# A hybrid SSD and forgetting-attention step on one core: weights times values in one fp32 product that also gives the sums, and row maxima from the high halves alone

## The chip, the cores and the metric

The kernel runs on one core of a Trainium2 chip. The metric is the device time of one execution in microseconds (us). The core has five engines that matter here: PE (matrix products; its weight loads are listed as PEld), DVE (vector), ACT (scalar functions), POOL (general purpose, also vector work) and the queues that issue DMA transfers, most of them on SP.

## The reference, cut to what matters

One inference step of a layer: a combined input projection, a Mamba-2 scan (8 heads) beside a forgetting attention (8 heads of 64), an output projection, a gated feed-forward part. The prompt has 2048 tokens, and 128 sample tokens (8 streams of 16) go with it. The change lies in the attention over the prompt, which is causal and has a per-token decay `F` added to the scores:

```python
def fox_block(q, k, v, fq, fk, q_pos, k_pos):
    s = jnp.einsum('bqhd,bkhd->bhqk', q, k).astype(jnp.float32) * FOX_SCALE
    s = s + (jnp.swapaxes(fq, 1, 2)[:, :, :, None] - jnp.swapaxes(fk, 1, 2)[:, :, None, :])
    s = jnp.where((k_pos[None, :] <= q_pos[:, None])[None, None], s, -jnp.inf)
    p = jax.nn.softmax(s, axis=-1)
    return jnp.einsum('bhqk,bkhd->bqhd', p.astype(v.dtype), v)
```

Everything is fp32.

## The kernel before

**Precision.** Most large products run in the format fp32r, on operands split into a high and a low half (`split`, L103 to L108: a cast to fp32r gives the high half, a subtraction the low one). A product of two split operands takes three fp32r products. A few small products (the scan's, L504, L511, L514, and transposes) run on plain fp32 operands.

**Stages.** The prompt goes through the input projection and the mixers in four parts of 512 tokens (p = 0 to 3). For each part `a_head` normalises, `a_body` projects (L116 to L118 and L346 to L348), and `attention(p, others)` runs the part's 8 heads, with chunks of the scan (`ssd_chunk`) between. The output projection (L819 to L821) begins while the attention of p = 3 runs. The feed-forward part (L116 to L118 with `wr`, L919 to L921) follows. The framework's scheduler decides in which order the instructions of these strands stand on each engine; each engine then runs its own list in order, and waits where something is not ready.

**Attention.** Scores of a block of 512 queries (`qb`) against a block of 512 keys (`kb`) are worked out twice.

- `s_phase` puts queries on the partitions, for the softmax's maximum and sum: for each of 4 groups of 128 queries two products (L589 over 128 rows, L590 over 68 rows: 64 dimensions and four rows for the decay and, later, the maximum), a maximum over the keys on DVE (L593), and an exponential with its sum on ACT (L594). At the end (L596 to L621) the maxima and sums of the blocks are joined, turned (L613), written to DRAM and read back: the maximum as two more rows of the queries, the reciprocal of the sum as `rdb`, spread over 64 partitions.
- `t_phase` puts keys on the partitions: for each of 4 groups of 128 keys two products (L646, L647), an exponential on ACT that gives the weights `pr` (L653), a split of the weights into `pp` by DVE (high, L107) and POOL (low, L108), and, two groups later, `weigh`: two products (L635) of the values with the high and with the low half of the weights. The stationary operand has the values' high half in 64 columns and their low half in the other 64, so the two halves of the accumulator `pv` are added at the end (L662, L663) and multiplied by `rdb` (L664).

Below, a unit is one such group of 128 keys (and beside it one of 128 queries): 8 heads times 4, 8, 12 and 16 units in the four parts, 320 in all. Of a head's diagonal block the four units are 512, 384, 256 and 128 columns wide, all others 512: 224 units of 512 and 32 each of 384, 256 and 128. `s_phase` runs ahead of `t_phase` by 4 units (`LEAD`), within one strand.

**Scan chunk.** `ssd_chunk` begins with `sg`, a difference of running sums for 8 heads, clipped at zero: 8 DVE instructions (L474), then an exponential.

## Time and profile before

| | |
|---|---|
| median of 3 runs | 3247.06 us (3239.56 to 3247.18) |
| the profiled execution, its time | 3243.1 us |
| its span, first to last instruction | 3241.4 us |
| PE busy | 3038.1 us (94%) |
| DVE, ACT, POOL busy | 2049.0, 1216.5, 1229.2 us |
| mean granted share of PE's clock | 0.969 |

The profile is of one execution. "Busy" of PE is the union of its instructions' spans, whose ends are modelled: a product of 512 columns lasts 0.39 us there while the next begins 0.23 us after it. The granted clock is the share of PE's full rate; it is either 1 (2.4 GHz) or 0.5 (1.2 GHz), and a value between is a mean over a stretch.

### The profile page before, as it was taken

To read this page: it belongs to the slowest core of one execution; us is meant where nothing else is said; L and a number is where in the kernel's file an instruction comes from. 1 tells how busy PE (TensorE), PEld (TensorE's weight loads), DVE (VectorE), ACT (ScalarE), POOL (GpSimd) and SP (SyncE) were. 2 spreads that over 40 slices of the span, in tenths; PEclk is the share of its full clock that TensorE was granted. 3 is DMA by queue.
4 is the path that set the end of the run, shared out by engine and by line. 5 is a ranking of instruction groups with operands and counts; after the bars stand their busy time and mean duration, and the time that the engine had idled before them with its cause. 6 is when DMAs were issued, how large, how long until landed. Compare 5 with 4: busy or idle time off the path is not lost.

```text
span 3241.4 us, 48271 instructions
## 1 busy us (share of the span) xinstructions
PE 3038.1 (94%) x18032; PEld 2741.7 (85%) x18032; DVE 2049.0 (63%) x3922; ACT 1216.5 (38%) x2442; POOL 1229.2 (38%) x803
## 2 busy tenths in 40 slices
PE   5988889799989997999899999999999999999999
PEld 5977788688878785886699999998999999999998
DVE  5376456867786777557555555556555555766666
ACT  3353344445555555434332222234222223322222
POOL 3343234554556556434333223233322323333332
PEclk9999989899989998998999999999999999999999
DMA  5767775676657656655432112123211212322221
GB/s 174 232 207 233 251 217 176 206 215 199 179 174 221 198 155 206 198 180 174 174 118 78 59 59 66 57 74 118 78 60 58 65 60 71 117 78 69 73 69 70
DMA packets 253458, 442.93 MB, mean 137 GB/s; under 512 B 24416, under 2 KB 121704, under 8 KB 253224
## 3 DMA queue, kind: packets, MB, share of 16 engines
q1 hardware_dynamic: 199656, 278.60, 27.6%
q10 hardware_dynamic: 53568, 161.24, 16.0%
q8 instruction: 143, 2.34, 0.3%
q14 instruction: 91, 0.75, 0.1%
HBM read 352.91 MB, written 86.84 MB: 136 GB/s over the span
## 4 chain that ended last, share of the span: by engine, by line
PE 70%; DMA 13%; DVE 10%; issue 3%; ACT 2%; POOL 2%; SPq 1%; ACTq 0%; DVEq 0%; POOLq 0%
PE mm L116 13%; PE mm L117 12%; PE mm L118 12%; PE dn L919 5%; PE dn L920 5%; PE dn L921 5%; PE pv L635 2%; DMA sg<-ac_d 2%; DVE pp L107 1%; PE dn L819 1%; PE dn L820 1%; PE dn L821 1%; DMA k<-k_d 1%; PE s L646 1%; PE s L589 1%
## 5 line engine op out<-in xcount | busy, mean ns | idle before, releaser
L108 POOL TENSOR_TENSOR wr<-raw,wr 128x1024 fp32r<-128x1024 f32 x198 | 475.9, 2411 | 1033.8 <-ACT wr L105 1025.5
L116 PE MATMUL mm<-nT,wr 128*128 128x386 f32 (+1 forms) x2112 | 697.0, 331 | 1.3 <-ACT wr L105 0.8
L117 PE MATMUL mm<-nT,wr 128*128 128x386 f32 (+1 forms) x2112 | 695.9, 330 | 0.1
L118 PE MATMUL mm<-nT,wr 128*128 128x386 f32 (+1 forms) x2112 | 695.2, 329 | 0.0
L108 POOL TENSOR_TENSOR pp<-pr,pp 128x512 fp32r<-128x512 f32 (+1 forms) x320 | 384.9, 1207 | 469.6 <-DVE pp L107 439.5
L897 DVE SCALAR_TENSOR_TENSOR ac<-mm,cw,ac 128x384 f32<-128x384 f32 (+1 forms) x528 | 301.8, 572 | 345.0 <-ACT ac L895 337.3
L895 ACT ACTIVATE ac<-mm,cw 128x384 f32<-128x384 f32 (+1 forms) x264 | 172.5, 653 | 786.5 <-PE mm L118 783.9
L922 DVE TENSOR_TENSOR y<-y,dn 128x512 f32<-128x512 f32 x374 | 255.4, 685 | 266.7 <-PE dn L921 263.9
L117 PEld LDWEIGHTS mm<-nT,wr 128*128 128x128 f32 x2112 | 399.9, 189 | 6.8 <-DVE nT L108 0.3
L116 PEld LDWEIGHTS mm<-nT,wr 128*128 128x128 f32 x2112 | 398.1, 189 | 7.7 <-ACT wr L105 1.1
L118 PEld LDWEIGHTS mm<-nT,wr 128*128 128x128 f32 x2112 | 398.3, 189 | 5.7
L108 POOL TENSOR_TENSOR cmw<-craw,cmw 128x1024 fp32r<-128x1024 f32 (+1 forms) x96 | 234.6, 2446 | 256.1 <-ACT cmw L105 237.9
L116 PE MATMUL mm<-nT,cmw 128*128 128x256 f32 (+2 forms) x1024 | 310.8, 303 | 16.8 <-DVE qk L405 5.5
L118 PE MATMUL mm<-nT,cmw 128*128 128x256 f32 (+2 forms) x1024 | 306.8, 300 | 0.0
L117 PE MATMUL mm<-nT,cmw 128*128 128x256 f32 (+2 forms) x1024 | 306.8, 300 | 0.0
L919 PE MATMUL dn<-wr,ht 128*128 128x512 f32 x748 | 294.6, 394 | 2.9 <-DVE y L922 1.7
L920 PE MATMUL dn<-wr,ht 128*128 128x512 f32 x748 | 293.0, 392 | 0.0
L921 PE MATMUL dn<-wr,ht 128*128 128x512 f32 x748 | 290.4, 391 | 0.0
L635 PE MATMUL pv<-pp,v 128*128 128x512 f32 (+3 forms) x640 | 231.4, 405 | 50.0 <-DVE yl L663 17.4
L105 ACT CAST wr<-raw 128x1024 fp32r<-128x1024 f32 x198 | 203.2, 1042 | 173.7 <-PE dn L921 161.4
L594 ACT ACTIVATE s<-s,nm 128x512 f32<-128x512 f32 (+2 forms) x320 | 190.9, 597 | 153.9 <-DVE nm L593 145.2
L653 ACT ACTIVATE pr<-s 128x512 f32<-128x512 f32 (+1 forms) x320 | 167.8, 532 | 182.3 <-PE s L647 118.4
(299 smaller groups left out, 6008.6 us busy)
## 6 DMA issues: line engine op xcount, KB each, us to landing
raw<-in_w_up ACTq DMA_DIRECT2D x132, 512.0 KB
k<-k_d SPq DMA_DIRECT2D x160, 256.0 KB
raw<-in_w_down ACTq DMA_DIRECT2D x66, 512.0 KB
craw<-in_w_cm ACTq DMA_DIRECT2D x64, 512.0 KB
k<-k_d SPq DMA_DIRECT2D x160, 136.0 KB
v<-v_d SPq DMA_DIRECT2D x80, 256.0 KB
craw<-in_w_tm ACTq DMA_DIRECT2D x24, 512.0 KB
q_d<-qk SPq DMA_DIRECT2D x96, 128.0 KB
```

Source lines behind the costliest of these rows:

```text
L105: S.copy(hi, src)
L108: leng.tensor_sub(lo, src, hi.bitcast(F32))
L116: T.matmul(ps[:, :W], whi(k), wt[:, 0, k, :W], start=k == 0, stop=False)
L117: T.matmul(ps[:, :W], whi(k), wt[:, 1, k, :W], start=False, stop=False)
L118: T.matmul(ps[:, :W], wlo(k), wt[:, 0, k, :W], start=False, stop=k == n - 1)
L594: S.activation(ps[:, :W], ps[:, :W], AF.Exp, bias=nm[:, qi, kb:kb + 1], accum_out=dn[:, qi, kb:kb + 1])
L635: m = T.matmul(pv[:, of:512], vr[:, jj], pp[:, a, :512 - of], start=first and a == 0, stop=last and a == 1)
L897: V.scalar_tensor_tensor(ac[:, 0:n], ps[:, j:j + n], cw2[:, ct, j:j + 1], ac[:, 0:n], op0=ALU.mult, op1=ALU.add)
L919: T.matmul(ps, ht[:, 0, ts_], wd[:, 0, cc], start=x == 0, stop=False)
L920: T.matmul(ps, ht[:, 0, ts_], wd[:, 1, cc], start=False, stop=False)
L921: T.matmul(ps, ht[:, 1, ts_], wd[:, 0, cc], start=False, stop=x == len(g) - 1)
L922: V.tensor_add(ys_[c][:, cc], ys_[c][:, cc], ps)
```

## The change

- `weigh` becomes one product on plain fp32 operands: the weights `pr` as ACT wrote them, the values as 64 columns, and ones in the other 64 columns of the stationary operand, so that the other half of `pv` holds the sums of the weights. The split of the weights (`pp`, DVE and POOL) and of the values (`vs`, `v2_d`) goes. `load_v` reads 64 columns of the output `v` in pieces of 256 bytes (before: 512 bytes of `v2_d`), after POOL has set the ones.
- `s_phase` takes only the product of the high halves (68 rows), and only the maxima: no exponential, no sums. The maximum is thus that of approximate scores; it cancels in the quotient. `load_ks` loads 136 KB where `load_k` loaded 256 and 136.
- At the head's end ACT copies both halves of `pv`; after each second head DVE takes the reciprocal of the sums in 4 pieces of 128x128, and multiplies.
- In `ssd_chunk` one subtraction on POOL and one minimum on DVE stand for the 8 DVE instructions.
- The PSUM banks of `mm` (2) and `tp` (1) become one ring of 3; `pr` has 4 buffers for 3, `v` 3 for 2; rows of the stored halves change places (`q1_d`, `k1_d`, `k2_d`).

```diff
-PB = 3
+PB = 4
...
-        return psa.tile([P, 512], F32, tag="mm", name="mm", bufs=2)
+        return psa.tile([P, 512], F32, tag="mm", name="mm", bufs=3)
...
-        return psa.tile([P, 512], F32, tag="tp", name="tp", bufs=1)
+        return psa.tile([P, 512], F32, tag="mm", name="tp", bufs=3)
...
-                if c != SMP:
-                    vs = at([P, 4, 2, HD], "vs", 1, F32R)
-                    p4 = ps[:, 0:256].rearrange("p (h d) -> p h d", h=4)
-                    S.copy(vs[:, :, 0], p4)
-                    V.tensor_sub(vs[:, :, 1], p4, vs[:, :, 0].bitcast(F32))
-                    dS(v2_d[c][:, half * 4:half * 4 + 4], vs.bitcast(F32))
...
-        for h in range(8):
-            V.tensor_scalar(sg[:, h], sg[:, h], acs[:, c, h:h + 1], 0.0, op0=ALU.subtract, op1=ALU.min)
+        G.tensor_sub(sg, sg, acs[:, c].unsqueeze(2).to_broadcast([P, 8, P]))
+        V.tensor_scalar_min(sg, sg, 0.0)
...
+    def load_ks(h, kb):
+        ks = bt_([P, 512], "ks", 3, F32R)
+        dma(ks[0:68].bitcast(F32), k2_d[h, :, kb * 512:(kb + 1) * 512])
+        return ks
...
-        vr = bt_([P, 4, P], "v", 2, F32R)
-        dma(vr.bitcast(F32), v2_d[4 * kb:4 * kb + 4, :, h].rearrange("c p a d -> p c (a d)"))
+        vr = bt_([P, 4, P], "v", 3)
+        e = h % 2 * HD
+        G.memset(vr[:, :, HD - e:2 * HD - e], 1.0)
+        dma(vr[:, :, e:e + HD], o["v"][4 * kb:4 * kb + 4, :, h * HD:(h + 1) * HD].rearrange("c p d -> p c d"))
...
-                T.matmul(ps[:, :W], q12[:, 0, qs], k12[:, 0, :W], start=True, stop=False)
-                T.matmul(ps[:, :W], q12[0:68, 1, qs], k12[0:68, 1, :W], start=False, stop=kb != qb)
+                T.matmul(ps[:, :W], q12[0:68, 1, qs], ks[0:68, :W], start=True, stop=kb != qb)
...
-                S.activation(ps[:, :W], ps[:, :W], AF.Exp, bias=nm[:, qi, kb:kb + 1], accum_out=dn[:, qi, kb:kb + 1])
...
-            V.tensor_sub(nm[:, :, :nb], nm[:, :, :nb], M.unsqueeze(2).to_broadcast([P, 4, nb]))
-            S.activation(nm[:, :, :nb], nm[:, :, :nb], AF.Exp, scale=-1.0)
-            V.tensor_mul(dn[:, :, :nb], dn[:, :, :nb], nm[:, :, :nb])
-            V.tensor_reduce(rd[:, 2], dn[:, :, :nb], op=ALU.add, axis=AX.X)
...
-        V.reciprocal(rd[:, 2], rd[:, 2])
...
-        dma(rdb[(h % 2) * 64:(h % 2 + 1) * 64], st_d[h, qb, 2:3].to_broadcast([64, 512]))
...
-            for a in range(2):
-                m = T.matmul(pv[:, of:512], vr[:, jj], pp[:, a, :512 - of], start=first and a == 0, stop=last and a == 1)
-                pv_ins.append(m.ins)
+            m = T.matmul(pv[:, of:512], vr[:, jj], pr[:, :512 - of], start=first, stop=last)
+            pv_ins.append(m.ins)
...
-                pp = bt_([P, 2, 512], "pp", 3, F32R)
-                split(pr[:, :W], pp[:, 0, :W], pp[:, 1, :W], V, G)
...
-        S.copy(yl[rs], pv[ot])
-        V.tensor_add(yl[rs], yl[rs], pv[rs])
-        V.tensor_mul(yl[rs], yl[rs], rdb[rs])
+        S.copy(yl[rs], pv[rs])
+        S.copy(dn[rs], pv[ot])
         if e:
+            for a in range(4):
+                cc = slice(a * P, (a + 1) * P)
+                V.reciprocal(dn[:, cc], dn[:, cc])
+            V.tensor_mul(yl, yl, dn)
```

The scheduler lays all engines' lists out anew. In the two programs the same source lines have other numbers; the pairs are given below.

**PE at the end of the attention** (part p = 3, last head; `s` are scores of `t_phase`, `pv` is `weigh`, `dn` the output projection). Before:

```order
L646 MATMUL s<-q_15807,k_16469 128x512
L647 MATMUL s<-q_15807,k_16469 128x512
L635 MATMUL pv<-pp,v 128x512 x2
L646 MATMUL s<-q_15807,k_16469 128x512
L647 MATMUL s<-q_15807,k_16469 128x512
L635 MATMUL pv<-pp,v 128x512 x13
L819 MATMUL dn<-wo,mx 128x512
L820 MATMUL dn<-wo,mx 128x512
```

With the change (L629 and L630 are the scores, L618 is `weigh`, L804 to L806 are the output projection):

```order
L618 MATMUL pv<-pr,v 128x512 x2
L629 MATMUL s<-q_13610,k_14099 128x512
L630 MATMUL s<-q_13610,k_14099 128x512
L805 MATMUL dn<-wo,mx 128x512
L806 MATMUL dn<-wo,mx 128x512
L804 MATMUL dn<-wo,mx 128x512
L618 MATMUL pv<-pr,v 128x512 x2
L805 MATMUL dn<-wo,mx 128x512
L806 MATMUL dn<-wo,mx 128x512
```

Before, nothing of another strand is left to stand between the last products; now products of the output projection do.

**DVE at the joining of the maxima** (part p = 3; `nm`, `M`, `mh`, `rd` and `dn` are the tiles of `s_phase`, the others belong to the convolution and the scan). Before:

```order
L108 TENSOR_TENSOR mh<-M,mh 128x4
L601 TENSOR_TENSOR nm<-nm,M 128x16
L611 COPY rd<-mh 128x8
L442 SCALAR_TENSOR_TENSOR cth<-cth,cac 128x256
L373 SCALAR_TENSOR_TENSOR ev<-ev,mm 128x256
L603 TENSOR_TENSOR dn<-dn,nm 128x16
L604 TENSOR_REDUCE rd<-dn 128x4
L608 RECIPROCAL rd<-rd 128x4
L549 SCALAR_TENSOR_TENSOR yt<-yt,ss,ngB 128x256 x2
L373 SCALAR_TENSOR_TENSOR ev<-ev,mm 128x256
L615 COPY rr<-s 12x128
```

With the change (L592 is the row maximum, L597 joins the blocks):

```order
L592 TENSOR_REDUCE nm<-s 128x1
L597 TENSOR_REDUCE M<-nm 128x4
L105 CAST mh<-M 128x4
L106 TENSOR_TENSOR mh<-M,mh 128x4
L425 SCALAR_TENSOR_TENSOR cac<-mm,cw_214,cac 128x256
L541 SCALAR_TENSOR_TENSOR yt<-yt,ss,ngB 128x256 x2
L425 SCALAR_TENSOR_TENSOR cac<-mm,cw_214,cac 128x256 x2
L605 COPY rr<-s 8x128
```

The steps between the last maximum and the turn on PE are three; the five that made the sums are gone.

**POOL in a stretch of the attention** (`cmw` is the split of projection weights, `xe` and `sg` belong to the scan). Before:

```order
L108 TENSOR_TENSOR pp<-pr,pp 128x512 x4
L108 TENSOR_TENSOR cmw<-craw,cmw 128x1024
L108 TENSOR_TENSOR pp<-pr,pp 128x512 x2
L108 TENSOR_TENSOR cmw<-craw,cmw 128x1024
L108 TENSOR_TENSOR pp<-pr,pp 128x512 x3
L108 TENSOR_TENSOR pp<-pr,pp 128x384
L108 TENSOR_TENSOR pp<-pr,pp 128x256
L108 TENSOR_TENSOR cmw<-craw,cmw 128x1024
```

With the change:

```order
L568 MEMSET v 128x4x64
L106 TENSOR_TENSOR cmw<-craw,cmw 128x4x256
L491 TENSOR_TENSOR xe<-xd,te 128x512
L568 MEMSET v 128x4x64
L465 TENSOR_TENSOR sg<-sg,acs 128x1024
L106 TENSOR_TENSOR cmw<-craw,cmw 128x4x256
```

One subtraction per unit has left POOL; a memset per four units and the `sg` subtraction have come.

## Rows read from the trace of the kernel before

**Rows 1.** The profile's page: span, and the busy time of each engine with its share of the span.
```profile
span 3241.4 us, 48271 instructions
PE 3038.1 (94%) x18032; PEld 2741.7 (85%) x18032; DVE 2049.0 (63%) x3922; ACT 1216.5 (38%) x2442; POOL 1229.2 (38%) x803
```

**Rows 2.** Busy time by stretch of the execution (from:to in us, then its length), with the number of instructions; then the mean granted share of PE's clock, the busy share of the DMA engines, and GB/s. The stretches: attention of p = 0 and the sample streams; the rest of p = 0 to the first half of p = 3; second half of p = 3, two stretches; the passage; the feed-forward part.
```profile
75.00:440.00 365.00, 329.83 (x2553) 296.53 (x2552) 194.19 (x550) 147.74 (x360) 129.60 (x85) 0.95 0.76 232
440.00:1280.00 840.00, 737.85 (x4905) 645.71 (x4903) 625.68 (x1279) 433.01 (x1039) 447.53 (x318) 0.93 0.64 193
1280.00:1480.00 200.00, 199.63 (x998) 161.25 (x997) 123.51 (x233) 85.69 (x201) 72.75 (x64) 1.00 0.58 188
1480.00:1577.00 97.00, 82.53 (x374) 60.03 (x373) 66.03 (x111) 39.50 (x89) 51.90 (x43) 0.84 0.39 125
1577.00:1640.00 63.00, 60.59 (x288) 49.65 (x287) 31.37 (x49) 19.10 (x41) 6.85 (x13) 1.00 0.69 247
1640.00:3241.00 1601.00, 1588.28 (x8666) 1491.26 (x8666) 964.85 (x1588) 467.02 (x668) 495.34 (x250) 1.00 0.23 73
```
Its columns are PE, PEld, DVE, ACT and POOL.

**Rows 3.** Groups of PE instructions by line and shape: count, then busy us and mean ns of one, then idle time of PE just before them and what ended it.
```profile
L635 PE MATMUL pv<-pp,v 128*128 128x512 f32 x448 | 181.9, 441 | 35.1 <-DVE yl L663 17.4 <-POOL pp L108 13.1 <-DVE pp L107 3.9
...
L589 PE MATMUL s<-k,q 128*128 128x512 f32 x224 | 95.2, 427 | 1.3 <-ACT s L594 1.2 <-DVE bs L485 0.2
```

**Rows 4.** Timeline of PE at two places: start us, length us, line, shape, count. L511 is a plain fp32 product of the scan (two in the program, of 256 columns each, here four records); the others are fp32r.
```profile
1544.04 1.03 PE L511 MATMUL s<-sst,xb 128*128 128x256 f32 x4
1544.72 0.58 PE L635 MATMUL pv<-pp,v 128*128 128x512 f32 x1
...
1560.51 0.40 PE L647 MATMUL s<-q,k 68*128 68x512 f32 x1
1560.74 0.40 PE L646 MATMUL s<-q,k 128*128 128x512 f32 x1
1560.98 0.40 PE L647 MATMUL s<-q,k 68*128 68x512 f32 x1
```

**Rows 5.** Timeline of PE, and of POOL, at the last units of the attention; in brackets the idle time before and what ended it.
```profile
1568.31 0.73 PE L635 MATMUL pv<-pp,v 128*128 128x512 f32 x2 [0.68 <-POOL pp L108]
1569.75 0.73 PE L635 MATMUL pv<-pp,v 128*128 128x512 f32 x2 [0.71 <-POOL pp L108]
...
1565.37 9.83 POOL L108 TENSOR_TENSOR pp<-pr,pp 128x512 fp32r<-128x512 f32 x7
```

**Rows 6.** Waits of PE and of its weight loads between 75 and 1640 us: who waited for whom, us in total, times, the longest.
```profile
PE pv L635 <- DVE yl L663: 17.4, 7, 4.3
PE pv L635 <- POOL pp L108: 16.4, 23, 2.5
PE pv L635 <- DVE pp L107: 15.2, 15, 3.8
PE s L613 <- DVE rd L608: 10.6, 8, 3.8
PE s L589 <- ACT s L594: 6.1, 8, 2.6
PE mm L116 <- DVE qk L405: 5.5, 4, 3.6
PE s L647 <- DMA k<-k_d: 3.2, 2, 2.6
...
PEld pv L635 <- POOL pp L108: 30.6, 37, 3.1
PEld pv L635 <- DVE pp L107: 21.1, 22, 4.0
```

**Rows 7.** Groups of POOL, DVE and ACT instructions by line, columns as in rows 3 ("+1 forms": the widths are together, so a mean is over them); then for L228 and L608 (the kernel's reciprocals) the count and the shortest, median and longest duration in ns.
```profile
L108 POOL TENSOR_TENSOR pp<-pr,pp 128x512 fp32r<-128x512 f32 (+1 forms) x320 | 384.9, 1207 | 469.6 <-DVE pp L107 439.5 <-ACT ev L356 6.7 <-DVE mh L108 5.0
L108 POOL TENSOR_TENSOR cmw<-craw,cmw 128x1024 fp32r<-128x1024 f32 x88 | 213.5, 2428 | 246.1 <-ACT cmw L105 228.0 <-DMA k_d<-qk 7.3 <-ACT ev L412 5.7
...
L107 DVE CAST pp<-pr 128x512 fp32r<-128x512 f32 (+1 forms) x320 | 197.2, 621 | 61.5 <-ACT pr L653 55.2 <-PE pv L635 4.5 <-ACT s L594 0.3
L594 ACT ACTIVATE s<-s,nm 128x512 f32<-128x512 f32 (+2 forms) x320 | 190.9, 597 | 153.9 <-DVE nm L593 145.2 <-DMA q<-q_d 4.7 <-DMA k<-k_d 1.4
L653 ACT ACTIVATE pr<-s 128x512 f32<-128x512 f32 x224 | 132.3, 597 | 154.2 <-PE s L647 118.4 <-PE s L649 21.2 <-POOL pp L108 12.7
L594 ACT ACTIVATION_READ_ACCUMULATOR s<-s,nm 128x1 f32 x320 | 63.5, 198 | 0.0
L474 DVE TENSOR_SCALAR sg<-sg,acs 128x128 f32<-128x128 f32 x136 | 37.6, 345 | 31.8 <-DMA sg<-ac_d 31.6
L663 DVE TENSOR_TENSOR yl<-yl,pv 64x512 f32<-64x512 f32 x32 | 21.8, 682 | 12.0 <-ACT yl L662 11.6
L662 ACT COPY yl<-pv 64x512 f32<-64x512 f32 x32 | 18.6, 580 | 11.7 <-PE pv L635 10.0 <-PE s L590 1.2
...
L228 DVE RECIPROCAL g_s<-g_s x4: 546/553/653, 62.1 to 946.7; 128x64 f32<-128x64 f32 x3, 128x80 f32<-128x80 f32 x1
L608 DVE RECIPROCAL rd<-rd x32: 159/178/179, 129.9 to 1537.3; 128x4 f32<-128x4 f32 x32
```

**Rows 8.** SP's waits before it could issue a load of values (as in rows 6), and the first DMA queue: packets, MB, and the time its packets took as a share of 16 engines' span.
```profile
SPq L569 <- PE pv L635: 83.4, 30, 7.4
...
q1 hardware_dynamic: 199656, 278.60, 27.6%
```

More of the change, by code (lines that the diff above doesn't have):

```diff
@@ L84, in hybrid_step @@
     ac_d = dram.tile([NTILE, H, P], F32, name="ac_d")
-    st_d = dram.tile([H, 4, 3, 512], F32, name="st_d")
-    v2_d = dram.tile([NTILE - 1, P, H, 2, HD], F32, name="v2_d")
+    st_d = dram.tile([H, 4, 2, 512], F32, name="st_d")
     sf_d = dram.tile([2, NB, H, PAST], F32, name="sf_d")
@@ L419, in f @@
                     hi, lo = (sp[e * 64:(e + 1) * 64, a].bitcast(F32) for a in range(2))
[L420 to L422 removed]
+                    dS((k1_d if kind else q1_d)[h, 0, :, tt], hi if kind else lo)
+                    dS((k1_d if kind else q1_d)[h, 1, :, tt], lo if kind else hi)
+                    dS((k2_d if kind else q2_d)[h, 0:64, tt], hi)
             return f
@@ L581, in s_phase @@
         nm = bt_([P, 4, 4], "nm", 2)
[L582 removed]
         for kb in range(qb + 1):
[L584 removed]
+            ks = load_ks(h, kb)
             for qi in range(4):
@@ L593, in s_phase, with t_phase @@
                 V.tensor_reduce(nm[:, qi, kb:kb + 1], ps[:, :W], op=ALU.max, axis=AX.X, negate=True)
[L594 removed]
                 yield
         nb = qb + 1
[L597 to L598 removed]
         if nb > 1:
+            M = bt_([P, 4], "M", 2)
             V.tensor_reduce(M, nm[:, :, :nb], op=ALU.min, axis=AX.X)
[L601 to L608 removed]
+        else:
+            M = nm[:, :, 0]
         mh = bt_([P, 2, 4], "mh", 2, F32R)
         split(M, mh[:, 0], mh[:, 1], V, V)
[L611 removed]
         pt = pss()
[L613 to L615 removed]
+        T.transpose(pt[0:8, 0:128], mh.rearrange("p a c -> p (a c)").bitcast(F32), ident)
+        rr = bt_([8, P], "rr", 2)
+        V.tensor_copy(rr, pt[0:8, 0:128])
         dS(st_d[h, qb].rearrange("a (c p) -> (a c) p", p=P), rr)
[L617 to L624 removed]
+        dma(q12[66:68, 1].bitcast(F32), st_d[h, qb])
+        done.append(q12)
     pv_ins = []
[L627 removed]
+    def t_phase(h, qb, q12, yl, dn):
         pv = psb.tile([P, 512], F32, tag="pv", name="pv", bufs=1)
@@ L630, in t_phase, with weigh @@
         late = []
-        def weigh(vr, jj, of, pp, first, last):
-            for a in range(2):
-                m = T.matmul(pv[:, of:512], vr[:, jj], pp[:, a, :512 - of], start=first and a == 0, stop=last and a == 1)
-                pv_ins.append(m.ins)
+        def weigh(vr, jj, of, pr, first, last):
+            m = T.matmul(pv[:, of:512], vr[:, jj], pr[:, :512 - of], start=first, stop=last)
+            pv_ins.append(m.ins)
         for kb in order:
@@ L653, in t_phase @@
                 S.activation(pr[:, :W], ps[:, :W], AF.Exp)
-                pp = bt_([P, 2, 512], "pp", 3, F32R)
-                split(pr[:, :W], pp[:, 0, :W], pp[:, 1, :W], V, G)
-                late.append((vr, jj, of, pp, kb == qb and jj == 0, kb == order[-1] and jj == 3))
+                late.append((vr, jj, of, pr, kb == qb and jj == 0, kb == order[-1] and jj == 3))
                 yield
@@ L690, in attention @@
                 yl = bt_([P, 512], "yl", 2)
-            for _ in t_phase(h, p, *done[h], yl):
+                dn = bt_([P, 512], "rdb", 2)
+            for _ in t_phase(h, p, done[h], yl, dn):
                 next(ahead, None)
```

20 lines of the change are left out of this document (removed).

## The prediction

> **What bounds the kernel now.** Read first the engines' shares [rows 1]: PE is busy 94% of the span, DVE 63%, ACT and POOL 38% each. That is a mean over stages, so the next view is the stretches [rows 2]. The feed-forward part, 1640 to 3241 us, has PE busy 1588 of 1601 us at full clock: the change doesn't touch it, and it keeps its time. The stretch before 75 us holds no products of the attention and is taken as unchanged. All that can move lies between 75 and 1640 us.
>
> There, PE's idle time is, stretch by stretch, 35.2 + 102.2 + 0.4 + 14.5 + 2.4 = 155 us, and PE's clock is low for part of the rest: length times the missing share of the clock is 18.3 + 58.8 + 0 + 15.5 + 0 = 93 us [rows 2]. The two go together: the stretch 1280 to 1480 us, with next to no gap, has a clock of 1.00, and 1480 to 1577 us, where PE stands 14.5 of 97 us, has 0.84. So PE is the bound, but of these 1565 us up to 155 + 93 = 248 are not work at full rate. DVE, over the same five rows, is busy 1041 us, ACT 725, POOL 709: none is full, so PE's gaps are waits in chains through several engines, and the table of waits [rows 6] says which. The largest group is the weighing, L635: it waits for POOL's and DVE's split of the weights (16.4 + 15.2 us as PE sees it, 30.6 + 21.1 as the weight loads, which stand a little earlier, see it), and at a head's start for L663 to free the accumulator (17.4). The clearest picture is the last units of the attention [rows 5]: PE does two products and stands 0.7 us; the pairs begin 1.44 us apart, and POOL runs 7 subtractions in 9.83 us, 1.40 each, without a pause. There the split on POOL sets the pace.
>
> **The change part by part.** The sum is made against the profiled execution's own 3243.1 us (4 us, 0.1%, under the median of 3247.06, and inside the three runs).
>
> *Weighing, PE.* The 320 units are 224 of 512 columns and 32 each of 384, 256 and 128, the width of 224 + 32 x 768/512 = 272 full units. An fp32r product of 512 columns takes its place on PE for 0.235 us (begin to begin, 1560.51 to 1560.98 for two [rows 4]), so two per unit now cost 272 x 0.47 = 128 us. The trace has no fp32 product of 512 columns; the nearest row is L511, 256 columns. Two program products stand there as four records, and the next product begins 0.68 us after the first and is shown 0.58 us long where its like is 0.40 [rows 4]: it really starts 0.18 us later. So 0.86 us for 512 columns. Bounds: 0.68 without that shift, and 1.03, the whole row. I take 0.86: 272 x 0.86 = 234 us, which is +106 (bounds +57 and +152).
>
> *Scores of the row maxima, PE.* L589 goes, 224 + 96 products [rows 3], the same 272 full widths x 0.235 = -64 us. So PE's work rises by 42 us (bounds -7 and +88). Nothing covers this where PE has no gap, as in 1280 to 1480 us.
>
> *The other engines are relieved.* DVE's 320 casts (197 us), POOL's 320 subtractions (385), ACT's 320 exponentials and the reads of their sums (191 + 64) go [rows 7]. None of it is a gain by itself; what PE waited for is:
>
> - *The split.* L635 waits for it 32 us in PE's view and 52 in the weight loads' [rows 6]. Now `weigh` needs only ACT's exponential, 0.60 us [rows 7], of the unit two groups before, during which PE has 1.6 us of work per unit. I take -40.
> - *A bank held by L594* (6.1 us): the exponential in PSUM is gone; DVE's maximum still frees the bank. I take -7 with the weight loads' part.
> - *L613 behind the reciprocal* (10.6 us): in the order of DVE five of the eight steps vanish. I take -9.
> - *The accumulator's release* (17.4 us): 0.58 on ACT and 0.68 on DVE become two copies of 0.58 on ACT [rows 7], an engine with a third less to do. I take -5, between 0 and -15.
> - *All other waits*: 155 less the 66 us listed in these four points is 89 us, in small rows: L405 freeing a bank, transfers of keys [rows 6], the scan's chain. DVE loses about a quarter of its load, ACT a third, POOL nearly half, and the ring of three banks gives the projections one more. I take a quarter, -22; bounds 0 and three quarters, -67.
>
> Together -83 us.
>
> *The clock.* With 83 of 155 us of gaps gone, 54% of the 93 us would follow if low clock went with gaps in proportion. Long gaps outside the attention's chain, which cost most clock, are not touched; I take -45, bounds 0 and -75.
>
> *Costs beside PE.* DVE's reciprocals: 0.55 us for 64 columns and 0.18 for 4 [rows 7], so about 6.2 ns a column, 0.95 us for a piece of 128; 4 x 16 pieces are 61 us of DVE, behind which row maxima of the next units queue for 3.8 us at a time. DVE still ends some 250 us lighter (the cast, the sums, L362, L663, L664 and L474 go), and the scores run 4 units ahead, some 6 us of PE; I take nothing. Uncovered it would be 16 x 3.8 = 61 us. `sg`: 8 x 0.345 us on DVE become a POOL instruction like L108's of the same size, 2.4 us, and a minimum of about 1 us; 0.7 us longer, 17 times, at most 12 us if no product stood beside it; taken as nothing. `load_v`: the memset now waits on POOL for a free buffer, and the splits of projection weights queue behind it. Before, the load's issue waited so on SP, 83.4 us in all, 7.4 at the longest [rows 8]; with three buffers and a POOL that is half empty I take nothing, at most 83. Fewer bytes move: 80 loads of 256 KB, 32 stores of 256 KB of `v2_d`, half of the values; no wait of PE on DMA is large [rows 6], so no gain is taken. The swap of stored rows costs nothing: the same transfers.
>
> **Sum**: 3243.1 + 42 - 83 - 45 = 3157 us.
>
> **The rivals.**
>
> *PE nearly gapless.* The "other waits" go by three quarters, the accumulator's by 15, and the clock gives 75: 3243 + 42 - (40 + 7 + 9 + 15 + 67) - 75 = 3072 us. For it: DVE's casts at the end of the attention and POOL's subtractions alternate, and every DVE instruction of the mixers queues between them. Against it: waits of the start of each part and of the sample streams have nothing to do with the split. By the Trainium skill (SBUF — State Buffer, section "SBUF: two separate sides") DVE and GpSimd lock a shared port pair for a whole instruction; POOL's 385 us of subtractions would then also have lengthened DVE's, which speaks for this rival; no row here tells a lock from a queue.
>
> *Slower: the waits only change their name.* PE runs its list in order; the chain from scores by exponential to weighing stays, and each weighing product is now 0.86 us that cannot be passed. If PE then waits at L618 for ACT, or at the scores for DVE's long reciprocals and maxima, as long as it waited for the split, only the 42 us remain: 3285 us. It decides if less than 42 of the 248 us, a sixth, come back. For it: DVE's row maximum stays, and 61 us of reciprocals are new. Against it: in [rows 5] the wait is plainly POOL's own pace of 1.40 us, which is gone.
>
> *The values come late.* Each of 80 loads now moves pieces of 256 bytes. The number of pieces (80 x 512) is as before; 199,656 packets in 27.6% of 16 engines' span are 72 ns each [rows 8]. At the same time per piece nothing changes; at twice, 40,960 x 72 ns / 16 = 184 us of all DMA engines, a share of 0.12 over these 1565 us beside the 0.64 now [rows 2], less what keys save: not full. But a load that lands late stops L618. The two waits for `k` are 1.6 us each [rows 6]; half of the loads late by that much would be 64 us: 3157 + 64 = 3221 us. The Trainium skill (DMA: Bandwidth & Descriptors, section "Specifications") gives 512 bytes as the least transfer for full rate, with read-modify-write below it; that speaks against the change, and no row here shows pieces of 256 bytes.
>
> **How the numbers follow.** Forecast near 3157: 0.60, its own range 3105 to 3210 (the bounds of waits and clock; the price of an fp32 product moves it by some 48 us either way). Nearly gapless: 0.20. Late values: 0.07. Waits that change their name: 0.13. A measurement of this kernel tells about 0.3%, 10 us, from no change. The first two are faster, 0.80, and about 0.02 of the third; 0.05 (the rest of the third, and forecasts where the fp32 price is at its upper bound) lies within 10 us; slower is 0.13. The range 3060 to 3235 leaves out the slower rival and half of the gapless one.
>
> **What would show it.** In the profile of the changed kernel: L618 begin to begin 0.86 us at 512 columns, two records each; L635's waits for POOL and DVE gone from the table and none of their size at L618; DVE between 75 us and the end of the attention near 790 us, POOL below 400, ACT near 480; PE's idle time there about 70 us instead of 155, its clock about 0.97; the feed-forward part again 1600 us; the reciprocals near 0.95 us. The prediction is wrong if fp32 products cost more than 1 us, if a wait of over 40 us stands at L618 (for ACT, for `v`, or for a memset), or if the clock stays at 0.94 although the gaps close.

## The result and the profile after

The changed kernel takes 3204.3 us (median of four executions, 3197.9 to 3210.1), the kernel before beside it 3244.9 (3239.6 to 3247.2). The ratio is 0.9877, with an interval of 0.9853 to 0.9900: 41 us faster, 1.2%. The prediction had 86 us: the sign and the range held, the size is missed by half.

The profiled execution of the changed kernel took 3197.9 us. The page's head, as in [rows 1]:

```profile
span 3196.2 us, 45570 instructions
PE 3030.4 (95%) x17712; PEld 2671.9 (84%) x17712; DVE 1787.8 (56%) x3315; ACT 1029.7 (32%) x1778; POOL 899.0 (28%) x580
```

Busy time by stretch, with the columns of [rows 2]. The feed-forward part now begins at 1594 us.

```profile
0.00:75.00 75.00, 25.62 (x151) 22.98 (x152) 41.42 (x110) 20.36 (x36) 25.92 (x34) 0.90 0.41 142
75.00:440.00 365.00, 337.80 (x2578) 300.79 (x2577) 166.79 (x464) 130.75 (x277) 102.83 (x62) 0.93 0.69 214
440.00:1280.00 840.00, 769.57 (x4897) 623.87 (x4896) 478.28 (x945) 323.94 (x633) 247.16 (x189) 0.95 0.55 168
1280.00:1480.00 200.00, 200.00 (x956) 147.77 (x955) 95.78 (x150) 56.49 (x107) 18.98 (x33) 0.99 0.48 155
1480.00:1594.00 114.00, 108.58 (x469) 85.54 (x468) 40.58 (x60) 30.15 (x58) 7.45 (x14) 0.97 0.49 176
1594.00:3196.00 1602.00, 1588.81 (x8669) 1490.98 (x8667) 964.98 (x1589) 467.98 (x668) 496.68 (x250) 1.00 0.23 73
```

From 75 us to the feed-forward part PE's idle time is 27.2 + 70.4 + 0 + 5.4 = 103 us (before 155). By the prediction's count, length times the missing share of the clock, the low clock costs 25.6 + 42.0 + 2.0 + 3.4 = 73 us (before 93). That count also takes in low clock while PE stands, which is idle time already. Below, the clock's cost is therefore PE's busy time times the missing share, added up over windows of 1 us: 53 us here, 73 before. Ahead of 75 us PE stands 14 us longer: 25.62 us busy against 39.35. The balance of the spans: idle -51.6 + 13.7, clock -21, and the rest, +14, is work; together -45, the difference of 3196.2 and 3241.4.

Waits of PE between 75 and 1594 us, and two of POOL's, as in [rows 6]; L618 is the new weighing, L589 and L630 are scores, L344 is a projection, L568 the memset of ones:

```profile
PE s L630 <- DMA q<-st_d: 15.9, 3, 8.5
PE s L757 <- ACT pr L751: 10.5, 4, 3.2
PE s L589 <- DVE rr L605: 8.8, 2, 6.4
PE mm L344 <- ACT nT L103: 7.5, 4, 4.3
PE mm L344 <- DVE xT L202: 6.6, 3, 3.8
...
PE s L629 <- DMA v<-out_v: 3.9, 1, 3.9
POOL v L568 <- PE pv L618: 251.2, 45, 15.8
POOL v L568 <- issue: 56.3, 10, 8.0
```

The weighing's waits for the split and for the accumulator are gone, and nothing of their size stands at L618. The groups that answer to [rows 3] and [rows 7] (for L648, count and shortest, median, longest in ns):

```profile
L618 PE MATMUL pv<-pr,v 128*128 128x512 f32 (+3 forms) x640 | 291.9, 548 | 2.6 <-issue 1.4 <-ACT pr L636 1.2
L589 PE MATMUL s<-ks,q 68*128 68x512 f32 (+2 forms) x320 | 147.3, 470 | 17.4 <-DVE rr L605 8.8 <-DVE nm L592 5.0 <-DMA v<-out_v 2.2
L465 POOL TENSOR_TENSOR sg<-sg,acs 128x1024 f32<-128x1024 f32 x17 | 32.7, 1922 | 106.6 <-DMA sg<-ac_d 41.8 <-DMA out_v<-ev 18.1 <-PE s L506 13.3
L648 DVE RECIPROCAL rdb<-rdb x64: 882/895/954, 201.0 to 1515.5; 128x128 f32<-128x128 f32 x64
```

Timeline of PE where nothing waits, columns as in [rows 4]: one fp32 weighing (two records) between fp32r products.

```profile
1406.75 0.39 PE L630 MATMUL s<-q,k 68*128 68x512 f32 x1
1406.98 1.02 PE L618 MATMUL pv<-pr,v 128*128 128x512 f32 x2
1407.44 0.80 PE L806 MATMUL dn<-wo,mx 128*128 128x512 f32 x1
1408.07 0.39 PE L804 MATMUL dn<-wo,mx 128*128 128x512 f32 x1
```

From the weighing's begin to that of the second product behind it are 1.09 us; less one fp32r product of 0.23 leaves 0.86 us, the price that the sum used.

### The profile page after: what moved, and what is told of

It reads as the page before. It is cut to its first block, busy times and chain, and to the rows that moved or that the text cites. A ratio compares the mean times of both kernels' runs of the same rounds, so it can differ in the third digit from the quotient of the medians.

```text
span 3196.2 us, 45570 instructions
## 1 busy us (share of the span) xinstructions
PE 3030.4 (95%) x17712; PEld 2671.9 (84%) x17712; DVE 1787.8 (56%) x3315; ACT 1029.7 (32%) x1778; POOL 899.0 (28%) x580
## 3 DMA queue, kind: packets, MB, share of 16 engines
q1 hardware_dynamic: 180712, 234.48, 23.3%
## 4 chain that ended last, share of the span: by engine, by line
PE 83%; DMA 10%; DVE 4%; issue 1%; SPq 1%; ACT 1%; POOL 0%; ACTq 0%; DVEq 0%; POOLq 0%
PE mm L115 14%; PE mm L114 14%; PE mm L116 14%; PE pv L618 6%; PE dn L904 5%; PE dn L905 5%; PE dn L906 5%; PE s L629 2%; PE s L630 2%; PE dn L804 2%; PE dn L805 2%; PE dn L806 2%; PE mm L346 2%; PE s L589 2%; PE mm L344 2%; PE mm L345 2%
## 5 line engine op out<-in xcount | busy, mean ns | idle before, releaser
L618 PE MATMUL pv<-pr,v 128*128 128x512 f32 (+3 forms) x640 | 291.9, 548 | 2.6 <-issue 1.4
L592 DVE TENSOR_REDUCE nm<-s 128x1 f32<-128x512 f32 (+2 forms) x320 | 190.9, 603 | 122.0 <-PE s L589 72.1
L636 ACT ACTIVATE pr<-s 128x512 f32<-128x512 f32 (+1 forms) x320 | 166.1, 532 | 267.9 <-PE s L630 198.6
L114 PEld LDWEIGHTS mm<-nT,cmw 128*128 128x128 f32 x1024 | 196.6, 192 | 8.8 <-issue 4.8
```

What stands on the lines that cost most here:

```text
L114: T.matmul(ps[:, :W], whi(k), wt[:, 0, k, :W], start=k == 0, stop=False)
L592: V.tensor_reduce(nm[:, qi, kb:kb + 1], ps[:, :W], op=ALU.max, axis=AX.X, negate=True)
L618: m = T.matmul(pv[:, of:512], vr[:, jj], pr[:, :512 - of], start=first, stop=last)
```

## The experiments

Each ratio is to the kernel before, timed in turn with it on the same chip; "faster" and "slower" are differences of medians to it. Its own median lay between 3239 and 3245 us in the sets.

### The banks: one ring or two

After the change, the projections (`mm`) and the small products of gates and norm (`tp`) take the same three banks in turn. The first test undoes that alone:

```diff
-        return psa.tile([P, 512], F32, tag="mm", name="mm", bufs=3)
+        return psa.tile([P, 512], F32, tag="mm", name="mm", bufs=2)
...
-        return psa.tile([P, 512], F32, tag="mm", name="tp", bufs=3)
+        return psa.tile([P, 512], F32, tag="tp", name="tp", bufs=1)
```

> The changed kernel, with one thing undone: the PSUM banks of the projections (mm, 2) and of the small products (tp, 1) are two rings again instead of one of 3. Theory R (the one ring holds the gates' small products and the second projection of values in one order, so PE stands beside the gates' chain at the start): PE's idle time in the first 100 us falls by about 20 us, the first product of t_phase begins near 150 us instead of 176, and the kernel takes 15 to 30 us less than with the change, about 3180. Theory N (the late start is the scheduler's chance, or the third bank earns elsewhere what it costs here): within 10 us of the changed kernel, 3195 to 3215, or slower.

Measured: 3158.4 us, ratio 0.9747 [0.9729, 0.9764], 85 us faster than before. One ring costs 44 us in the changed kernel. Its stretches, columns as above:

```profile
0.00:75.00 75.00, 44.73 (x300) 42.85 (x301) 41.90 (x110) 24.29 (x43) 30.83 (x36) 0.93 0.49 163
75.00:440.00 365.00, 322.86 (x2403) 282.20 (x2402) 180.40 (x473) 124.06 (x271) 96.29 (x59) 0.91 0.68 208
440.00:1280.00 840.00, 795.73 (x5074) 645.22 (x5074) 500.12 (x972) 334.02 (x655) 251.78 (x198) 0.97 0.59 175
1280.00:1480.00 200.00, 200.00 (x924) 148.61 (x923) 82.21 (x124) 54.02 (x99) 16.22 (x26) 1.00 0.45 151
1480.00:1558.00 78.00, 75.44 (x351) 62.67 (x350) 31.94 (x49) 20.40 (x42) 4.82 (x13) 0.98 0.56 197
```

PE idles 42.1 + 44.3 + 0 + 2.6 = 89 us here, the clock costs 49 us (60 by the prediction's count), and PE has 19 us more behind it at 75 us than with one ring.

The same ring given to the kernel before (its two `bufs` lines changed the other way):

> The kernel before, with one part of the change alone: one ring of 3 banks for mm and tp. Theory R: the first product of t_phase begins about 25 us later than in the kernel before, and the time rises by 10 to 30 us, to about 3265. Theory N: within 10 us of 3245, or faster.

Measured: 3255.6 us, ratio 1.0032 [1.0017, 1.0048]: 10 to 12 us slower. In neither kernel is it a help.

Where does it cost? The first theory was the start, as the rows of 0 to 75 us suggest (25.62 us busy with one ring, 44.73 with two), and as the first scores of the weighing phase begin 54 us later (176 against 122 us). Two kernels take the three banks in turn in the first part alone (below), or in all others (there `p > 0`); the rest has two and one:

```diff
+    def bank(name, p):
+        if p == 0:
+            tag = ("mm", "mm", "tp")[nb_[0] % 3]
+            nb_[0] += 1
+        else:
+            tag = name
+        return psa.tile([P, 512], F32, tag=tag, name=name, bufs=2 if tag == "mm" else 1)
```

> The changed kernel with its ring of three banks in the first part alone (projections and gates of part 0 take the three banks in turn); from the second part on two banks for the projections and one for the gates, as before. Ring throughout: 3204; two rings throughout: 3158. If the ring costs its 46 us at the start, where PE stands beside the gates' chain and the first attention begins 54 us later: 3190 to 3204. If it costs them within the attention, where a bank of the projections is held by a gate's small product: 3158 to 3170.

> The counterpart: two banks and one in part 0, the ring of three from the second part on. If the start holds the cost: 3158 to 3172. If the attention does: 3190 to 3204. If the two shares add, this and the ring at the start lie 46 us above 3158 together.

Measured: 3159.1 us (0.9744 [0.9728, 0.9760]) with the ring at the start, 3210.9 us (0.9901 [0.9886, 0.9916]) with it later. The theory of the start falls outright: with the ring at the start the late start is there, with PE 29.63 us busy ahead of 75 us,

```profile
0.00:75.00 75.00, 29.63 (x155) 26.05 (x155) 44.78 (x123) 20.16 (x36) 25.99 (x34) 0.81 0.41 142
75.00:440.00 365.00, 338.89 (x2611) 303.41 (x2610) 168.64 (x467) 129.51 (x278) 102.73 (x62) 0.95 0.70 215
440.00:1280.00 840.00, 794.24 (x5038) 641.60 (x5037) 503.05 (x971) 334.13 (x656) 250.44 (x197) 0.97 0.59 175
```

and it costs nothing. Products that PE could not do then fill what would have been gaps later: from 75 to 440 us PE is busy 338.89 us in this kernel, 322.86 with two rings. All of the loss stems from the second part on: the ring there alone costs 54 us against two rings, the ring throughout 44. The changed kernel starts as late as this one and from 75 us on has 28 us more idle time (103 against 75) and loses 14 us more to the clock (53 against 39). In the changed kernel the norm's products at a part's head (L196) show what happens there; the lines count those between 350 and 730 us, in the changed kernel and with two rings:

```profile
L196 PE MATMUL tp<-dg,ones x8: 270/275/377, 556.5 to 576.7; 128*128 128x128 f32 x8
```

```profile
L196 PE MATMUL tp<-dg,ones x12: 271/274/377, 393.0 to 692.2; 128*128 128x128 f32 x12
```

With a bank of its own the head of a part's first window runs some 160 us ahead, and so does that of the next part, which ends the second line (692); in one ring the head of the first window stands right behind the last projection of the part before, the next part's first projections (24 products for each of 4 tiles, which the gates need) among and behind the heads, and all others behind the gates. In the changed kernel no projection runs between these two, 40 us apart, with all the gates' products (from 649.59 us on) between them:

```profile
627.35 0.29 PE L346 MATMUL mm<-cmw,nT 128*128 128x272 f32 x1
667.57 0.60 PE L280 MATMUL tp<-ident,g_nh 128*8 128x128 f32 x4
667.92 0.37 PE L344 MATMUL mm<-cmw,nT 128*128 128x256 f32 x1
```

With two rings projections run beside the gates (624.6 to 640.0 us there). The projections' products alone (tiles `mm`; here the columns are PE, PEld, DVE, ACT), in the changed kernel and with two rings:

```profile
550.00:650.00 100.00, 22.05 (x132) 18.91 (x132) 1.47 (x6) 2.15 (x6) 0.88 0.58 172
```

```profile
550.00:650.00 100.00, 53.45 (x351) 46.36 (x350) 3.55 (x11) 5.29 (x15) 0.98 0.60 189
```

and all of each kernel's engines in the same 100 us, in the same order:

```profile
550.00:650.00 100.00, 82.52 (x481) 61.00 (x479) 71.58 (x141) 40.47 (x87) 36.88 (x34) 0.88 0.58 172
```

```profile
550.00:650.00 100.00, 94.98 (x649) 78.69 (x648) 71.55 (x151) 42.23 (x91) 41.91 (x34) 0.98 0.60 189
```

The projections are what fills PE while the attention's chain waits. In one ring most of them are missing for this stretch, PE stands 17 us instead of 5, and the clock is 0.88 instead of 0.98.

Which of the two users of the third bank does it? Each was put alone into the projections' two banks, first the gates' products (`tpt()` to `mmt()` in `gates`, seven places), then the norm's (the one in `a_head`):

```diff
-        pc = tpt()
+        pc = mmt()
```

> The changed kernel with two banks for the projections and one beside them, but the gates' small products take the projections' two banks; the third bank serves the norm's products at a part's head alone (L196). Two rings: 3158; ring of three from part 1 on: 3211, where the head's products of the next part stand behind all projections of the part before (at 571 us, next at 919) and with own banks run 190 us ahead (at 393, next at 664). If that running ahead is what the ring takes away: 3158 to 3172, with L196 of part 2 near 390 us. If the gates' chain holding a bank of the projections is the cost: 3190 to 3215, with a stop of the projections near the gates' products.

> The counterpart of the gates in the projections' banks (3194): now the norm's products at a part's head take the projections' two banks, and the gates' small products have the third alone. Two rings: 3158. If the gates' products are needed for the loss, as the stop of the projections beside them says: 3158 to 3168. If the head's products cost as much when they cannot run ahead: 3190 or more. If the two shares add to the ring's 46 us: near 3170.

Measured: gates 3193.8 us (0.9853 [0.9825, 0.9880]), head 3183.2 us (0.9825 [0.9805, 0.9846]); against two rings 37 and 29 us, each uncertain by about 10. With the gates in the projections' banks the head runs ahead (first at 361.7 us) and the time is lost all the same; with the head there it does not (580.3). Either is enough for most of the loss, and the two don't add: 66 against 44 to 54 together. (With two shared banks where the ring has three, these runs may show each user's part too large.) So running ahead is not the whole cause, as the expectation of the gates' run would have had it; what both share, by their edits, is that projections wait for a bank that a chain through DVE holds.

That the ring from the second part on costs the time is shown. That it does so through held banks, and not through some other order that the scheduler came to, is argued: each of these kernels has its own lists. For it speak the stop that ends with the gates' last product, and the five kernels with a shared bank in the later parts, all slower than their partner (10 to 54 us), while the two without lie within 1 us of each other. So do PE's waits at the first projections of a part (L344, L346) for the head's chain through DVE, ACT and POOL: 14 us in the changed kernel, 6 with two rings.

### The two parts of the change alone

The scores' part on the kernel before (one product for the maxima, no exponentials; it leaves out the sums, so its attention output is not the right one):

```diff
-                T.matmul(ps[:, :W], q12[:, 0, qs], k12[:, 0, :W], start=True, stop=False)
-                T.matmul(ps[:, :W], q12[0:68, 1, qs], k12[0:68, 1, :W], start=False, stop=kb != qb)
+                T.matmul(ps[:, :W], q12[0:68, 1, qs], ks[0:68, :W], start=True, stop=kb != qb)
...
-                S.activation(ps[:, :W], ps[:, :W], AF.Exp, bias=nm[:, qi, kb:kb + 1], accum_out=dn[:, qi, kb:kb + 1])
```

> The kernel before, with the scores' part of the change alone: the row maxima from one product of 68 rows, no exponentials on the scores, no sums from them; the weighing stays two fp32r products of a split. Left out: the sums, so the values are divided by something that is no sum. Kernel before: 3243. By the steps of the prediction: PE -64, the bank held by the exponential -7, the turn behind the reciprocal -9, a part of the other waits -8, the clock in proportion 24/155 of 93 = -14: 3141. By the theory that PE's work counts at the rate that the return of the second product showed (38 us for 64): 3205. By the theory that the split of the weights on POOL at 1.40 us a unit sets the pace wherever the attention waits: over 3215.

The weighing's part, with the scores as before (the diff above, the other way, on the kernel with two rings):

> The kernel before, with the weighing's part alone (fp32 weights, ones beside the values, three value buffers, sg on POOL, banks of the projections as two and one); the scores as before with both products, exponentials and their sums, which are computed and then not used. By the steps of the prediction: PE +106, split -40, accumulator -5, others -10, clock 55/155 of 93 = -33: 3261. Counted down from the whole change with two rings (3158): second product and exponentials back at the rate shown (38) to full (64), and 16 us of waits for bank and turn: 3212 to 3238. If the two parts add, this time and that of the scores alone, less 3243, give 3158.

Measured: scores alone 3162.6 us (0.9767 [0.9746, 0.9787]), 77 faster; weighing alone 3212.1 us (0.9917 [0.9898, 0.9936]), 27 faster although it gives PE some 100 us more to do as priced. The 20 us that the two lack of adding (104 against 85) show in idle time and clock. Their largest stretch, scores alone first, then weighing alone:

```profile
440.00:1280.00 840.00, 742.51 (x4892) 647.51 (x4891) 685.37 (x1304) 314.41 (x633) 473.48 (x347) 0.93 0.61 186
```

```profile
440.00:1280.00 840.00, 800.31 (x5106) 651.86 (x5104) 490.52 (x1008) 460.58 (x1098) 239.82 (x187) 0.98 0.61 184
```

From 75 us to the feed-forward part, in us, each kernel's profiled execution (its span against that of before, 3241.4), and beside it the medians:

| kernel | PE idle | lost to the clock | work of PE against before | span against before | median against before |
|---|---|---|---|---|---|
| before | 155 | 73 | | | |
| scores alone | 140 | 70 | -67 | -85 | -77 |
| weighing alone | 84 | 33 | +85 | -32 | -27 |
| both, two rings | 89 | 49 | +14 | -81 | -85 |
| both, ring at the start | 75 | 39 | +14 | -87 | -82 |
| both, one ring (the change) | 103 | 53 | +14 | -45 | -41 |

"Work" is PE's busy time over the whole execution less what the clock adds to it. The columns give the span together with the start, where idle time and clock are 13 us above before in the change and in the ring at the start, 5 to 7 below with two rings and in the weighing alone, and the same in the scores alone. The work is the same in the three kernels that have all of the change, and the parts' -67 + 85 = +18 agree with it, but the prices were -64 and +106. A part of the 21 to 28 us between is the modelled ends: a product before a gap is shown some 0.16 us longer than its place (0.39 for 0.23), and PE has 166 gaps before, 151 with the scores alone, 78 with the weighing alone and in the change, 72 with two rings. By that estimate some 14 or 15 us of the kernel before are idle time shown as work. The rest, 7 to 13 us, was not separated.

So the weighing's part is what closes the gaps (71 of idle, 40 of clock), and the scores' part is mostly plain work taken off PE.

What a change of PE's work brings when little else changes was tried from both sides. The changed kernel with the second product of the scores back, and with it its 256 KB for each load of keys:

```diff
-                T.matmul(ps[:, :W], q12[0:68, 1, qs], ks[0:68, :W], start=True, stop=kb != qb)
+                T.matmul(ps[:, :W], q12[:, 0, qs], k12[:, 0, :W], start=True, stop=False)
+                T.matmul(ps[:, :W], q12[0:68, 1, qs], k12[0:68, 1, :W], start=False, stop=kb != qb)
```

> The changed kernel, with the second product of the scores for the maxima put back (128 rows beside 68, and its 256 KB per load); no exponential comes back. It adds 272 full widths x 0.235 = 64 us to PE. Theory P (PE sets the pace of the attention nearly everywhere): slower by 50 to 65 us, about 3260. Theory W (PE's gaps in the chains swallow a good part of any PE work): slower by 20 to 40 us.

Measured: 3241.9 us (1.0000 [0.9989, 1.0012]), 38 us over the changed kernel for 64 us of work. And the weighing as one fp32r product, which leaves out the low halves of weights and values:

```diff
-        G.memset(vr[:, :, HD - e:2 * HD - e], 1.0)
...
+        G.tensor_copy(vr[:, :, HD - e:2 * HD - e], ones4)
...
+        G.tensor_copy(vr[:, :, e:e + HD], raw)
...
-                pr = bt_([P, 528], "pr", PB)
+                pr = bt_([P, 528], "pr", PB, F32R)
```

> The changed kernel with two rings, with the weighing as one fp32r product instead of one fp32 product: the low halves of weights and values are left out; POOL copies the values and the ones into an fp32r tile (two copies for each of 80 loads). It takes 272 x (0.855 - 0.235) = 169 us of PE away and nothing else. Changed kernel with two rings: 3158. If PE's own work is the bound throughout: 2989. At the rate that the scores' second product showed (0.59): 3058. If the chain from scores by exponential to weighing and the maxima on DVE take over as the bound: over 3110.

Measured: 3043.6 us (0.9397 [0.9375, 0.9420]), 111 us more below before than two rings alone (115 by the two medians), for 169 us of work: 0.66 to 0.68 us for each, between the first two theories and nearer to the second; the scores gave 0.59. PE is the bound, but not alone: with less to do its idle time grows again, in the largest stretch from 44 to 77 us.

```profile
440.00:1280.00 840.00, 762.88 (x5150) 672.53 (x5151) 542.23 (x1014) 353.76 (x693) 292.75 (x271) 0.95 0.62 190
```

### What is left in the kernel with two rings

Its largest wait is that of the weighing for the exponential (PE between 75 and 1558 us):

```profile
PE pv L618 <- ACT pr L636: 18.3, 6, 6.3
PE s L589 <- ACT pr L636: 8.2, 3, 3.9
PE s L589 <- DVE nm L592: 8.0, 3, 4.3
```

The weighing was put three units behind the scores instead of two:

```diff
-PB = 4
+PB = 5
...
-                if len(late) == 2:
+                if len(late) == 3:
```

> The changed kernel with two rings, with the weighing three units behind the scores instead of two, and five buffers for the weights instead of four. PE stands at L618 for ACT's exponential some 20 us over the whole attention in the kernel with two rings. If that wait is the exponential's depth: 3158 - 20, and some 5 of clock: 3133 to 3140. If the late exponential stems from ACT's other work, which comes in bursts longer than a unit, less than 8 us: 3150 to 3160.

Measured: 3141.5 us (0.9700 [0.9681, 0.9720]), 98 under before where two rings alone had 85. The gain is there, but the weighing's own wait hardly shrank:

```profile
PE pv L618 <- ACT pr L636: 15.2, 6, 6.8
PE s L629 <- ACT pr L636: 3.4, 2, 1.9
```

What shrank is the scores' wait for the same exponential, at L589 and L629 together from 14.7 us (8.2 above and 6.5 at L629) to 4.1, and the clock's loss (0.985 over the span against 0.980). The time is near the first expectation, its place is not where that looked for it.

With the scores of the maxima eight units ahead as well (`LEAD = 8`):

> Two rings, the weighing three units behind, five weight buffers (3141.5), and the scores of the maxima eight units ahead of the attention instead of four. Waits in the run with four ahead that it could take: the queries' row of maxima arriving late (9.8 us), the turn and the maxima (6.7 + 3.8). If these are the lead: 3141 - 15 = 3127, with clock 3122. If they come from DVE's queue, which is as long as before, 3136 to 3146.

Measured: 3135.4 us (0.9667 [0.9653, 0.9682]), 106 under before, and so the fastest that keeps all of the change's arithmetic; the 8 us over the run before it are about what two such measurements can tell.

The later weighing with one fp32r product:

> One fp32r weighing product (the low halves of weights and values left out) with two rings, as before 3043.6, and the weighing three units behind the scores with five weight buffers. PE waited there at L623 for the exponential (4.9 us) and in the scores for a bank held by the exponential (15.7). The later weighing takes only the first kind: 3033 to 3040. If what counts is the clock that short waits cost: down to 3025.

Measured: 3048.4 us (0.9402 [0.9388, 0.9416]): no gain over 3043.6, so the small gain above isn't to be had where the weighing is short.

The decays of the mixers back on DVE:

```diff
-        G.tensor_sub(sg, sg, acs[:, c].unsqueeze(2).to_broadcast([P, 8, P]))
-        V.tensor_scalar_min(sg, sg, 0.0)
+        for h in range(8):
+            V.tensor_scalar(sg[:, h], sg[:, h], acs[:, c, h:h + 1], 0.0, op0=ALU.subtract, op1=ALU.min)
```

> The changed kernel with two rings, with the decays of the mixers as before: eight instructions on DVE instead of one on POOL and one on DVE. The prediction took the move as nothing, at most 12 us. By it: 3150 to 3166. If DVE, lighter by 250 us, had been worth relieving here as well: 3164 to 3175. If the POOL instruction of 2.4 us stood in the chain of the mixers: 3146 to 3152.

Measured: 3165.3 us (0.9765 [0.9729, 0.9802]), 7 to 11 us over two rings with an interval of 12 either way. That tells nothing apart: it fits the prediction, which took the move as nothing, and does not show it.

## Why the prediction was right, and where it was wrong

**The step that failed** is in "All other waits": "the ring of three banks gives the projections one more", counted among the reasons for -22. The ring gives them one more bank, and with it the later parts lose 44 to 54 us: a help was counted where the runs show a cost. That projections stand behind the gates' and the norm's products is the reading of it (above). With two rings the changed kernel takes 3158.4 us, where 3157 was forecast; the ring's 44 us are as large as the whole miss. The step could have been seen as an open one: the change was in the diff, no row of before shows what waits behind a shared bank, and so a loss had to be priced as a bound.

**"The stretch before 75 us ... is taken as unchanged"** was wrong as a fact (14 us more idle) and right as a price: the run with the ring at the start shows that this loss is made good later.

**The agreement with two rings is in part luck: errors inside it cancel.** Against +42 of work, -83 of waits and -45 of clock, the table and the start give about +14, -71 and -24. With the 15 us of modelled ends moved from work to idle time (estimate above) they are +29, -86 and -24: the waits as forecast, the work 13 lower and the clock 21 less than forecast, which cancel but for 8. Of the clock's, the starting figure is a part: of the 93 us, 19 to 20 are low clock while PE stood, which the 155 us of idle time hold already, so that 228 and not 248 us were free to win. Nor did the clock follow the idle time in proportion: 75 to 440 us has 0.91 with two rings and had 0.95 before, with 42 us of idle time for 35. In the change as made the clock gave 21 us for 45, the waits 37 for 83.

**Waits by name.** The split (-40) and the bank held by L594's exponential (-7) left the list as forecast, though with two rings L589 waits 8.2 us for a bank that the other exponential, L636, holds. The accumulator's wait, 17.4 us, is not in the list any more, where -5 was taken and -15 was the bound. The turn's 10.6 us (-9) are 4.3 at L603, but 8.8 stand at the scores for the copy behind it, L605. The weighing's part as a whole removed more than its terms said: 71 us of idle and 40 of clock where split, accumulator, its share of the others and clock in proportion make 88 in the expectation of that run. The scores' part removed less: 77 with 64 of work as priced leaves 13 for waits and clock (18 in the profiled execution), where 38 had been expected. The two were sized as if they added, and they lack 20 us of it.

**What should show it.** The price of the fp32 product held (0.86). DVE's time in the moved stretches, 166.79 + 478.28 + 95.78 + 40.58 = 781 us, was forecast near 790; POOL's, 376, below 400; ACT's is 541 where 480 was forecast: the accumulators' reads, 64 us in [rows 7], can't all have been time of their own: with the exponentials' 191 they make 255, less some 19 for the 32 copies that came, and ACT's whole busy time fell by 187. The reciprocals are 0.895 us for 0.95. PE's idle time is 103 us (89 with two rings) instead of about 70, and its clock (1519 - 73)/1519 = 0.95 instead of 0.97: by the prediction's own list this was the sign that it is off.

**The rivals.** "The waits only change their name" needs waits at L618 or the scores as long as those for the split; the list shows 15.9 and 8.8 us at the scores for the stored maxima and the copy ahead of them, and 1.2 at L618. So part of the waits did change their name, but it didn't decide: 37 us of idle time and 21 of clock came back, start included, more than the 42 that it allows. The near gapless case did not come either. "The values come late" did not happen: 180712 packets in 23.3% of 16 engines' time of 3196 us are 66 ns each, against 72 before [rows 8],

```profile
q1 hardware_dynamic: 180712, 234.48, 23.3%
```

and the time per piece, which the rival needed doubled, fell. The trace's packets by size: 40,960 of 256 bytes in the changed kernel have a median of 18 ns, those of 512 bytes in both kernels 27. The 72 ns that the prediction took for a piece are a mean over all sizes; 2048 bytes take 84, 4096 take 159. PE's waits put down to `v` are 3.9 us at L629 and 2.2 at L589. The Trainium skill (DMA: Bandwidth & Descriptors, section "Specifications") puts the least transfer for full rate at 512 bytes. Here no step stands at 512: the time grows evenly with the size (18, 27, 84, 159 ns as above), 512 bytes move at 19 bytes a ns and 4096 at 26, so a smaller piece does cost rate, which agrees; but 512 bytes are not at the full rate either, and the measurement decides. POOL waits 251 us for value buffers in front of the memset, three times as long as SP did for its loads [rows 8]; of that no more than the 6 us above reaches PE's waits, as the prediction took it.

DVE did gain from a quieter POOL, which the prediction left open. DVE's row maximum, which reads PSUM, keeps its median of 679 ns. But L549 (L541 after), whose operands all lie in SBUF, has a median of 484 ns before, a longest of 2579 and a mean of 882; the mean is 1061 in the scores alone, 552 in the change and 480 in the weighing alone. In the kernel before 13 of its 34 last over 600 ns, and each of these ends 0.28 us after a POOL subtraction ends; the other 21 last at most 485. Two L549 in a row in the kernel before, and POOL beside them:

```profile
1276.05 2.98 DVE L549 SCALAR_TENSOR_TENSOR yt<-yt,ss,ngB 128x256 f32<-128x256 f32 x2 [6.81 <-POOL ss L112]
1276.25 2.50 POOL L108 TENSOR_TENSOR wo<-raw,wo 128x1024 fp32r<-128x1024 f32 x1 [0.23 <-ACT wo L105]
```

What is long is the instruction itself while POOL's runs, and not its wait: that is a lock, where the prediction had no row to tell it from a queue. Over the seven DVE groups of this kind that were compared (L549, L442, L541, L540, L515, L108's `mh`, L233) it is 140 us of DVE's time before and 110 in the change; what of it reached PE was not tried by itself.

## What to carry to other kernels

Buffers merged into one ring can also merge the orders of their users: before counting the extra buffer as a help, ask which slow chain now holds a buffer that the filler work needs. A late start that shows in the first slices need not cost anything when the work it delays fills later gaps, so place a loss by undoing it in one part of the program before explaining it. And a kernel whose bound engine is 95% busy returns, here, 0.6 to 0.7 us for each us of work taken off it.

## What the runs showed of the hardware

An fp32 product of 512 columns takes 0.86 us of PE at full clock in this kernel, two records in the trace, where the fp32r product takes 0.235: 3.7 times. The Trainium skill (FP8 and Floating Point Precision, section "TensorE Precision Notes") counts four passes for true fp32; the measured 3.7 is near that. POOL did the subtraction with a broadcast operand over 128x1024 in 1.92 us, where its subtractions of the same size with a rounded output take 2.43 [rows 7]. DVE's reciprocal of 128x128 takes 0.895 us, 7.0 ns a column, the fixed part included. A DVE instruction whose operands all lie in SBUF, 484 ns in the median, lasted up to 2579 ns while a POOL subtraction ran, and ended 0.28 us after it, in the kernel before 13 times out of 13; DVE's maxima out of PSUM did not stretch (longest 693 ns). A DMA packet took 18 ns for 256 bytes, 27 for 512, 84 for 2048 and 159 for 4096, medians.
